# A two-layer hybrid block whose instruction order is planned with the frame's timeline simulation

## The chip, the cores and the metric

One core of one Trainium2 chip runs the whole kernel. The metric is device time in microseconds of one execution; the figure for a kernel is the median of its runs.

## The reference

Two layers over 512 tokens of width 1024, 256 of context and 256 latent, in fp32. Each layer is FFN, token mix, FFN. The mix sends one normalised input through a projection `w_in`, whose parts feed four branches and four sigmoid gates:

```python
h = modulate(rms_norm(x, g_pre), mod[:, :, 3 * j], mod[:, :, 3 * j + 1])
return x + FFN_RES_WEIGHT * mod[:, :, 3 * j + 2] * rms_norm(swiglu(h, w1, w3, w2), g_post)
...
h_lat = modulate(rms_norm(x_lat, norm_pre[layer, 1]), mod_lat[:, :, 3], mod_lat[:, :, 4])
ya_l, ya_c = s5_branch(zl[0], zc[0], *s5_p, with_ctx_out)
yb_l, yb_c = mla_branch(zl[1:4], zc[1:4], *mla_p, rope_b, with_ctx_out)
yc_l, yc_c = hgrn_branch(zl[4:9], zc[4:9], *hgrn_p, with_ctx_out)
yd_l, yd_c = gqa_branch(zl[9:12], zc[9:12], *gqa_p, rope_d, with_ctx_out)
...
merged = gates[:, :, 0] * (branches[0] @ w_branch[0])
for i in range(1, N_BRANCH):
    merged = merged + gates[:, :, i] * (branches[i] @ w_branch[i])
return merged @ w_out
```

After each sub-layer the result is normalised, scaled and added to `x`. Layer 1 gives only the latent tokens out.

## The kernel before

Activations lie transposed, 128 channels to a partition block and tokens along the free axis; a 1024-channel tensor is eight tiles of 128x512. Every large matrix product is made of three fp32r matmuls (`mm3`, L346 to L348): each operand is split into a high part, cast on ScalarE (ACT; `whi` L318 for weights, `hh` L566 for the input), and a low part, the difference, on VectorE (DVE; `wlo` L319, `hl` L567). Weights stream from HBM in pieces of 128x1024 through three raw buffers and four pairs of split buffers; a cast waits until the matmuls that read its buffer's last piece are through.

The program is a sequence of FFN, mix, FFN, twice. Between two of them stands a `turn`: the last pieces of the old output are multiplied for the first half of the tokens and then for the second; for each half the sums of squares (`sqa` L587, L593) go through ones-matmuls (`st` L304) into a small tile; two reciprocal square roots of eleven operations of 128x2 each (L292 to L297, three rounds of Newton) follow one another, with `sx` (L616 to L619) between them; their results are spread over the partitions by matmuls (`rb` L311) and copied by ACT (`rbs` L313). Then `x` is updated (`ay` L632, `x` L633) and the next input is made (`ht` L564, `hh` L566, `hl` L567), eight blocks of each:

```python
t = self.u("ht")
nc.vector.scalar_tensor_tensor(
    t[:, a:b], self.x[kb][:, a:b], sc[:, kb, v : v + 1], rs, op0=ALU.mult, op1=ALU.mult)
nc.scalar.activation(hh[:, a:b], t[:, a:b], AF.Identity, bias=sh[:, kb, v : v + 1])
nc.vector.scalar_tensor_tensor(
    hl[:, a:b], t[:, a:b], sh[:, kb, v : v + 1], hh[:, a:b].bitcast(F32), op0=ALU.add, op1=ALU.subtract)
```

The first four pieces of the next stage's weights are loaded and split ahead of their use (`self.ahead`, L319 inside the turn). There are four full turns, and a last one with the latent half alone. In the mix, each branch is a lane of short matmuls with ACT and DVE steps between them; the gate projections (`pj`, 24 matmuls of 256 columns a piece in layer 1) are written between the lanes' steps as fillers. HGRN runs in two directions (`hgrn0`, `hgrn1`): in a direction, `hs` and `hb` belong to the output norm of the one before, `ckt`, `cst`, `clv`, `cdg` to its chunks, `oc` is its output. The S5 branch ends with `s5o`, the transposes `yt`, a gate product `gz` and the branch product `br` (L346 to L348).

The code is written in one order, with a priority for each instruction. The frame (`tile.TileContext`) then plans, for each engine, the order in which its instructions stand in the engine's queue: it takes the instructions that are ready by its own idea of durations, the more urgent first. Each engine executes its queue in that order and waits on semaphores for the others. The profile's line L1869 is the place where the frame is opened.

## Time and profile before

| | |
|---|---|
| median of 3 runs | 2361.51 us (2357.76 to 2361.8) |
| the profiled execution | 2360.09 us, span 2358.2 us |
| mean granted TensorE clock | 0.983 of full |
| PE (TensorE) busy | 2266.5 us, 96% |
| DVE busy | 1635.1 us, 69% |
| ACT busy | 903.0 us, 38% |
| HBM traffic | 326.79 MB by DMA, mean 139 GB/s |

The span is the time from the first instruction to the last; the profiled execution's own time has 1.9 us more around it. A share is an average over stages, and PE's records overlap where matmuls are pipelined.

### The profile page before, as it was taken

The numbers are of one execution on the slowest core, as the hardware profiler recorded it, in microseconds if no ns is written. First come the engines' busy times: TensorE is split into PE (matmuls) and PEld (weight loads), VectorE is DVE, ScalarE is ACT, GpSimd is POOL, SyncE is SP. The second block draws the span as 40 slices with busy tenths as digits, with TensorE's granted clock in tenths as the row PEclk, the third lists the DMA queues.
The fourth block names the chain that finished last, engine by engine and source line by source line (L and its number), as shares of the span: only waits on it lengthen the run. The fifth ranks groups of instructions, "written<-read, shape, count | busy, mean of one in ns | idle before, by whom it ended". The sixth has DMA issues, their size and how long they took to land.

```text
span 2358.2 us, 38797 instructions
## 1 busy us (share of the span) xinstructions
PE 2266.5 (96%) x15188; PEld 1903.8 (81%) x15188; DVE 1635.1 (69%) x4024; ACT 903.0 (38%) x1548; POOL 53.3 (2%) x116
## 2 busy tenths in 40 slices
PE   7999999999999999989999999999998999998998
PEld 4778779977557778888887898888897877888997
DVE  5887675756665574899776468777767886777554
ACT  3322323454443323542332333232234564345443
POOL 0000020000000000000002000000000000000000
PEclk9999999999999999999999999999998999998999
DMA  7545554221541243235555325656533332454664
GB/s 245 174 156 162 187 179 130 83 86 55 173 138 41 86 148 94 72 126 161 187 189 155 100 81 164 192 171 194 173 117 92 102 112 64 150 171 128 185 186 134
DMA packets 105270, 326.79 MB, mean 139 GB/s; under 512 B 16192, under 2 KB 17984, under 8 KB 105088
## 3 DMA queue, kind: packets, MB, share of 16 engines
q1 hardware_dynamic: 96448, 306.00, 42.2%
q0 software_dynamic: 4032, 9.93, 1.2%
q10 hardware_dynamic: 4608, 8.39, 1.0%
q8 instruction: 119, 1.95, 0.3%
q14 instruction: 63, 0.52, 0.1%
HBM read 311.20 MB, written 15.17 MB: 138 GB/s over the span
## 4 chain that ended last, share of the span: by engine, by line
PE 82%; DVE 10%; DMA 3%; ACT 3%; issue 2%; SPq 0%; DVEq 0%; ACTq 0%
PE h L346 10%; PE h L348 10%; PE h L347 10%; PE y L346 6%; PE y L348 6%; PE y L347 6%; PE pj L346 5%; PE pj L348 5%; PE pj L347 5%; DVE wlo L319 2%; PE s L896 2%; DMA araw<-in_w_adaT_dram 2%; ACT whi L318 1%; PE od L923 1%; PE tk L348 1%
## 5 line engine op out<-in xcount | busy, mean ns | idle before, releaser
L318 ACT CAST whi<-raw 128x1024 fp32r<-128x1024 f32 x402 | 421.4, 1050 | 805.8 <-DMA raw<-in_ffn_dram 288.1
L319 DVE TENSOR_TENSOR wlo<-raw,whi 128x1024 fp32r<-128x1024 f32 x402 | 490.9, 1223 | 285.4 <-ACT whi L318 283.4
L346 PE MATMUL h<-hh,whi 128*128 128x512 f32 (+1 forms) x1472 | 526.4, 359 | 11.1 <-DVE gf L687 3.9
L348 PE MATMUL h<-hh,wlo 128*128 128x512 f32 (+1 forms) x1472 | 525.3, 358 | 8.6 <-DVE wlo L319 8.6
L347 PE MATMUL h<-hl,whi 128*128 128x512 f32 (+1 forms) x1472 | 524.4, 357 | 0.0
L346 PEld LDWEIGHTS h<-hh,whi 128*128 128x128 f32 x1472 | 281.3, 192 | 55.5 <-issue 4.4
L348 PEld LDWEIGHTS h<-hh,wlo 128*128 128x128 f32 x1472 | 281.3, 192 | 50.9 <-DVE wlo L319 8.8
L347 PEld LDWEIGHTS h<-hl,whi 128*128 128x128 f32 x1472 | 281.7, 192 | 38.2
L346 PE MATMUL pj<-hh,whi 128*128 128x256 f32 (+1 forms) x800 | 276.5, 348 | 3.3 <-ACT hh L566 2.7
L348 PE MATMUL pj<-hh,wlo 128*128 128x256 f32 (+1 forms) x800 | 274.3, 345 | 4.4 <-DVE wlo L319 4.4
L347 PE MATMUL pj<-hl,whi 128*128 128x256 f32 (+1 forms) x800 | 275.3, 345 | 0.0
L346 PE MATMUL y<-gh,whi 128*128 128x256 f32 (+1 forms) x726 | 240.7, 332 | 2.8 <-ACT t L686 2.5
L348 PE MATMUL y<-gh,wlo 128*128 128x256 f32 (+1 forms) x726 | 241.2, 332 | 0.0
L347 PE MATMUL y<-gl,whi 128*128 128x256 f32 (+1 forms) x726 | 240.7, 332 | 0.0
L348 PEld LDWEIGHTS pj<-hh,wlo 128*128 128x128 f32 x800 | 153.7, 193 | 24.9 <-DVE wlo L319 6.0
L346 PEld LDWEIGHTS pj<-hh,whi 128*128 128x128 f32 x800 | 153.9, 193 | 23.5 <-issue 5.2
L347 PEld LDWEIGHTS pj<-hl,whi 128*128 128x128 f32 x800 | 154.2, 193 | 18.4 <-issue 3.9
L346 PEld LDWEIGHTS y<-gh,whi 128*128 128x128 f32 x726 | 137.9, 190 | 16.2 <-ACT t L686 2.7
L348 PEld LDWEIGHTS y<-gh,wlo 128*128 128x128 f32 x726 | 137.9, 190 | 13.0
L347 PEld LDWEIGHTS y<-gl,whi 128*128 128x128 f32 x726 | 137.9, 190 | 12.9
L425 DVE SCALAR_TENSOR_TENSOR aj<-araw,cr 128x512 f32<-128x512 f32 x112 | 77.2, 689 | 55.4 <-DMA araw<-in_w_adaT_dram 55.0
L688 ACT CAST gh<-gf 128x512 fp32r<-128x512 f32 (+1 forms) x88 | 49.8, 566 | 148.4 <-DVE gf L687 148.1
(413 smaller groups left out, 3263.0 us busy)
## 6 DMA issues: line engine op xcount, KB each, us to landing
raw<-in_ffn_dram SPq DMA_DIRECT2D x267, 512.0 KB, 4.0
araw<-in_w_adaT_dram SPq DMA_DIRECT2D x104, 512.0 KB, 4.1
raw<-in_win_dram SPq DMA_DIRECT2D x102, 512.0 KB, 3.7
araw<-in_w_ada_dram SPq DMA_DIRECT2D x24, 512.0 KB, 3.8
raw<-in_wout_dram SPq DMA_DIRECT2D x17, 512.0 KB, 3.6
raw<-in_wbr_dram SPq DMA_DIRECT2D x16, 512.0 KB, 3.7
araw<-in_w_ada_dram SPq DMA_DIRECT2D x22, 256.0 KB, 5.5
s5G<-s5g POOLq DMA_DIRECT2D x16, 256.0 KB, 3.1
```

Of the source, the lines that this page charges most:

```text
L318: self.nc.scalar.copy(hi, src)
L319: self.nc.vector.tensor_tensor(lo, src, hi.bitcast(F32), op=ALU.subtract)
L346: mm(ps, wh, xh, start=start, stop=False, skip_group_check=True)
L347: mm(ps, wh, xl, start=False, stop=False, skip_group_check=True)
L348: mm(ps, wl, xh, start=False, stop=stop, skip_group_check=True)
L425: nc.vector.scalar_tensor_tensor(w if v else junk, w, 1.0, S[v], op0=ALU.mult, op1=ALU.mult, accum_out=t[:, 2 * op + i, v : v + 1])
L688: nc.scalar.copy(gh[:, a:b], gf[:, a:b])
L896: nc.tensor.matmul(s[:, :w], q[:, j * P : (j + 1) * P], k[:, :w], start=True, stop=True)
L923: nc.tensor.matmul(out[n][64 * h : 64 * h + 64, j * P : (j + 1) * P], vh(kb), ph[:, kb * P : (kb + 1) * P], start=kb == 0, stop=kb == nk - ...
```

## The change

```diff
-    with tile.TileContext(nc) as tc:
+    with tile.TileContext(nc, schedule_with_timeline_sim=True) as tc:
         build(tc, aps, out)
```

The instructions, tiles, pools and priorities stay as they are. The frame's plan now takes the times of its timeline simulation, so the queues come out in another order: on PE 13066 matmuls in both, on DVE 3592 instructions, on SyncE 672 DMAs. Three places follow.

The first place is DVE's queue in the turn behind the first FFN (the first turn). In the order before, the second reciprocal square root stands between the updates of `x`; the numbers behind the names are buffers, and `wlo_3753` is a weight of the old stage:

```order
L616 TENSOR_TENSOR sx_3620<-st_3594,ry_3602 128x2
L617 SCALAR_TENSOR_TENSOR sx_3620<-st_3594,sx_3620 128x2
L319 TENSOR_TENSOR wlo_3753<-raw_3750,whi_3752 128x1024
L618 TENSOR_TENSOR sx_3620<-sx_3620,ry_3602 128x2
L632 TENSOR_TENSOR ay_2842<-ay_2842,rbs_3615 128x256
L619 SCALAR_TENSOR_TENSOR sx_3620<-sx_3620,sx_199 128x2
L632 TENSOR_TENSOR ay_2854<-ay_2854,rbs_3615 128x256
L292 TENSOR_SCALAR rs_3625<-sx_3620 128x2
L633 TENSOR_TENSOR x_107<-x_107,ay_2842 128x256
L293 TENSOR_SCALAR ry_3626<-rs_3625 128x2
L633 TENSOR_TENSOR x_108<-x_108,ay_2854 128x256
L295 TENSOR_TENSOR rt_3627<-ry_3626 128x2
```

Still before, farther down in the same turn, the splits for the next stage (`wlo_3893`, `wlo_3899`, `wlo_3905`) stand behind the first half's last `hl`:

```order
L567 SCALAR_TENSOR_TENSOR hl_3588<-ht_3828,mod_3_642,hh_3587 128x256
L610 TENSOR_SCALAR sv_3846<-st_3838 128x2
L319 TENSOR_TENSOR wlo_3893<-raw_3890,whi_3892 128x1024
L567 SCALAR_TENSOR_TENSOR hl_3590<-ht_3834,mod_3_642,hh_3589 128x256
L292 TENSOR_SCALAR rs_3848<-sv_3846 128x2
L319 TENSOR_TENSOR wlo_3899<-raw_3896,whi_3898 128x1024
L293 TENSOR_SCALAR ry_3849<-rs_3848 128x2
L319 TENSOR_TENSOR wlo_3905<-raw_3902,whi_3904 128x1024
```

In the new order, at the place of the first of these pieces:

```order
L616 TENSOR_TENSOR sx_3620<-st_3594,ry_3602 128x2
L319 TENSOR_TENSOR wlo_3893<-raw_3890,whi_3892 128x1024
L617 SCALAR_TENSOR_TENSOR sx_3620<-st_3594,sx_3620 128x2
L618 TENSOR_TENSOR sx_3620<-sx_3620,ry_3602 128x2
L619 SCALAR_TENSOR_TENSOR sx_3620<-sx_3620,sx_199 128x2
L292 TENSOR_SCALAR rs_3625<-sx_3620 128x2
L293 TENSOR_SCALAR ry_3626<-rs_3625 128x2
L295 TENSOR_TENSOR rt_3627<-ry_3626 128x2
L296 SCALAR_TENSOR_TENSOR rt_3627<-rt_3627,sx_3620 128x2
L319 TENSOR_TENSOR wlo_3899<-raw_3896,whi_3898 128x1024
L297 SCALAR_TENSOR_TENSOR ry_3626<-rt_3627,ry_3626 128x2
L632 TENSOR_TENSOR ay_2842<-ay_2842,rbs_3615 128x256
```

Two of those splits now stand inside the second root, whose small operations follow one another, and the eight L632 stand in one run behind them. The other two splits come between the L633 that follow; then come eight `ht` in a row and behind them the eight `hl`. The other three full turns read the same way, that behind the first mix a little differently.

The second place is PE's queue in layer 1's mix, at the start of the second HGRN direction. Before:

```order
L346 MATMUL pj_18043<-hh_16013,whi_18039 128x256
L347 MATMUL pj_18043<-hl_16014,whi_18039 128x256
L348 MATMUL pj_18043<-hh_16013,wlo_18040 128x256
L346 MATMUL pj_18043<-hh_16015,whi_18039 128x256
L1150 MATMUL ckt_17701<-cst,ckd_17681 128x128
L347 MATMUL pj_18043<-hl_16016,whi_18039 128x256
L348 MATMUL pj_18043<-hh_16015,wlo_18040 128x256
L1150 MATMUL ckt_17701<-cst,ckd_17681 128x128
L346 MATMUL pj_18043<-hh_16017,whi_18039 128x256
L347 MATMUL pj_18043<-hl_16018,whi_18039 128x256
L1150 MATMUL ckt_17701<-cst,ckd_17681 128x128
L348 MATMUL pj_18043<-hh_16017,wlo_18040 128x256
```

And in the new order, from the norm of the direction before:

```order
L346 MATMUL pj_18467<-hh_16021,whi_18463 128x512
L347 MATMUL pj_18467<-hl_16022,whi_18463 128x512
L348 MATMUL pj_18467<-hh_16021,wlo_18464 128x512
L865 MATMUL hb_17620<-cst,he_17621 128x128 x2
L1150 MATMUL ckt_17701<-cst,ckd_17681 128x128 x3
L1155 MATMUL cst_17707<-vc_16671,ckt_17702 64x64 x4
L1155 MATMUL cst_17707<-vc_16673,ckt_17702 64x64 x2
L1201 MATMUL clv_17754<-cx_17748 64x64
L1201 MATMUL clv_17755<-cx_17748 64x64
L1201 MATMUL clv_17754<-cx_17748 64x64
L1201 MATMUL clv_17755<-cx_17748 64x64
L1201 MATMUL clv_17775<-cx_17769 32x32 x4
```

The `pj` that stood between the `ckt`, `cst`, `clv` and `cdg` now stand ahead of `hb`; from there to the last `oc` there is none.

The third place is PE's queue at the end of layer 1's S5 branch. Before, the last `gz` is followed by 47 `pj` and then `br`:

```order
L347 MATMUL gz_19659<-yl_19646,gwh_19628 128x256
L348 MATMUL gz_19659<-yh_19645,gwl_19629 128x256
L347 MATMUL pj_20314<-hl_16008,whi_20310 128x256
L348 MATMUL pj_20314<-hh_16007,wlo_20311 128x256
L346 MATMUL pj_20314<-hh_16009,whi_20310 128x256
L347 MATMUL pj_20314<-hl_16010,whi_20310 128x256
```

In the new order `br` follows at once:

```order
L348 MATMUL gz_19649<-yh_19645,gwl_19629 128x256
L347 MATMUL gz_19659<-yl_19646,gwh_19628 128x256
L348 MATMUL gz_19659<-yh_19645,gwl_19629 128x256
L346 MATMUL br_20387<-yh_20373,whi_20383 128x256
L346 MATMUL br_20396<-yh_20373,whi_20383 128x256
L346 MATMUL br_20405<-yh_20373,whi_20383 128x256
L347 MATMUL br_20387<-yl_20374,whi_20383 128x256
```

The same holds for the two joints ahead of it, from `s5o` to `yt` and from `yt` to `gz`: the five last groups of `pj` stand ahead of the last `s5o`.

## Rows read from the trace of the kernel before

**Rows 1.** The page: busy time by engine, and the chain that ended last.
```profile
PE 2266.5 (96%) x15188; PEld 1903.8 (81%) x15188; DVE 1635.1 (69%) x4024; ACT 903.0 (38%) x1548; POOL 53.3 (2%) x116
...
PE 82%; DVE 10%; DMA 3%; ACT 3%; issue 2%; SPq 0%; DVEq 0%; ACTq 0%
```

**Rows 2.** Turn windows: us; busy us (count) of PE, PEld, DVE, ACT, POOL; PEclk.
```profile
416.00:452.00 36.00, 31.32 (x245) 30.59 (x245) 33.46 (x121) 12.96 (x25) 1.32 (x3) 0.95 0.25 78
990.00:1029.00 39.00, 31.20 (x239) 30.68 (x239) 37.26 (x132) 16.23 (x34) 0.00 (x0) 0.87 0.22 68
1381.00:1417.00 36.00, 31.41 (x241) 30.67 (x240) 32.86 (x119) 12.75 (x25) 0.00 (x0) 0.91 0.26 74
1756.00:1793.00 37.00, 27.00 (x198) 26.01 (x197) 33.30 (x120) 12.77 (x25) 1.32 (x3) 0.85 0.25 76
2135.00:2165.00 30.00, 22.43 (x126) 20.55 (x125) 25.51 (x80) 11.42 (x24) 0.00 (x0) 0.66 0.28 88
```

**Rows 3.** Waits of PE: waited for, total us, times, longest us.
```profile
PE h L348 <- DVE wlo L319: 8.6, 2, 6.5
```

**Rows 4.** Timeline of DVE, first turn: start us, us, engine and line.
```profile
416.69 0.16 DVE L292 TENSOR_SCALAR rs<-sv 128x2 int32<-128x2 int32 x1
...
418.93 0.16 DVE L616 TENSOR_TENSOR sx<-st,ry 128x2 f32<-128x2 f32 x1
...
419.89 1.23 DVE L319 TENSOR_TENSOR wlo<-raw,whi 128x1024 fp32r<-128x1024 f32 x1 [0.61 <-ACT whi L318]
...
425.91 0.16 DVE L297 SCALAR_TENSOR_TENSOR ry<-rt,ry 128x2 f32<-128x2 f32 x1
...
425.98 0.76 DVE L632 TENSOR_TENSOR ay<-ay,rbs 128x256 f32<-128x256 f32 x2
...
426.65 0.76 DVE L633 TENSOR_TENSOR x<-x,ay 128x256 f32<-128x256 f32 x2
...
427.34 1.28 DVE L564 SCALAR_TENSOR_TENSOR ht<-x,mod,rbs 128x256 f32<-128x256 f32 x3
...
436.09 1.22 DVE L319 TENSOR_TENSOR wlo<-raw,whi 128x1024 fp32r<-128x1024 f32 x1
```

**Rows 5.** Timeline of PE, first turn.
```profile
431.40 0.28 PE L348 MATMUL y<-gh,wlo 128*128 128x256 f32 x1
...
437.37 0.58 PE L348 MATMUL pj<-hh,wlo 128*128 128x256 f32 x1 [2.13 <-DVE wlo L319]
...
451.84 0.74 PE L346 MATMUL pj<-hh,whi 128*128 128x256 f32 x4 [1.17 <-ACT hh L566]
```

**Rows 6.** Windows: a turn's first half, a stall, HGRN, S5 tail.
```profile
437.40:448.90 11.50, 11.50 (x85) 11.50 (x86) 10.35 (x41) 1.42 (x2) 1.32 (x3) 0.86 0.63 194
1010.60:1020.80 10.20, 5.10 (x24) 5.10 (x25) 9.66 (x30) 2.97 (x5) 0.00 (x0) 0.50 0.33 92
1890.60:1936.00 45.40, 43.87 (x588) 36.47 (x588) 39.52 (x122) 30.73 (x80) 0.00 (x0) 1.00 0.38 115
2088.80:2111.20 22.40, 22.31 (x188) 21.78 (x185) 14.73 (x22) 13.89 (x25) 0.00 (x0) 1.00 0.59 176
```

**Rows 7.** Groups by form in the HGRN stretch of layer 1: busy, mean.
```profile
L348 PE MATMUL pj<-hh,wlo 128*128 128x256 f32 x65 | 19.0, 293 | 0.3 <-DVE wlo L319 0.3
...
L346 PE MATMUL pj<-hh,whi 128*128 128x512 f32 x11 | 4.5, 414 | 0.6 <-ACT gt L1676 0.6
...
L319 DVE TENSOR_TENSOR wlo<-raw,whi 128x1024 fp32r<-128x1024 f32 x10 | 12.2, 1220 | 1.1 <-ACT whi L318 1.0
```

**Rows 8.** Timelines of ACT and PE, S5 tail of layer 1.
```profile
2089.08 0.59 ACT L1617 ACTIVATE sq<-s5o 64x512 f32<-64x512 f32 x1 [0.47 <-PE s5o L1611]
...
2109.62 0.72 ACT L321 ACTIVATE yh<-gsg 128x256 fp32r<-128x256 f32 x2
...
2111.19 0.28 PE L346 MATMUL br<-yh,whi 128*128 128x256 f32 x1
```

**Rows 9.** Timeline of PE, layer 0, first br of S5.
```profile
944.59 0.96 PE L346 MATMUL br<-yh,whi 128*128 128x512 f32 x3 [1.92 <-ACT yh L321]
```

## Prediction

> **What bounds the kernel now.** I read the page first. TensorE (PE) is busy 2266.5 of 2358.2 us, VectorE (DVE) 1635.1, and 82% of the chain that ended last is PE [rows 1]. So the kernel is a PE stream with 91.7 us of holes, and an order that adds or takes away holes moves the end one for one; work that only changes place inside a full stretch is worth nothing. The view by windows then says where the holes are: the four full turns and the short last one hold 4.7 + 7.8 + 4.6 + 10.0 + 7.6 = 34.7 us of them, and there DVE is the fuller engine: 33.5 of 36 us, 37.3 of 39, 32.9 of 36, 33.3 of 37 [rows 2]. The longest single wait for a weight split lies in a turn, 6.5 us of PE's h matmuls [rows 3]. The other 57 us are thin: the first weights, the two mixes, the last output. In two stretches of layer 1's mix that the new order touches, PE has almost no hole: 43.87 of 45.4 us in the HGRN stretch, 22.31 of 22.4 in the S5 tail [rows 6].
>
> **The turn, in DVE's queue.** The change adds no work: the same instructions stand on PE and DVE. In a turn it moves four 128x1024 splits (wlo, L319) from behind the first half's hl to a place among the small rsqrt operations and the x updates; it puts all eight ht ahead of the first hl; and it takes the small operations out from between the large ones. I walk the first turn through.
>
> Prices [rows 4]: the eleven operations of a rsqrt, each waiting for the last, take 418.93 - 416.69 = 2.24 us, 0.20 each; one small operation ahead of a large one costs 0.07 (425.91 to 425.98); four large ones (L632, L633) take 427.34 - 425.98 = 1.36, 0.34 each; of three ht in 1.28 us each adds 0.40, and hl has the same shape; a split busy for 1.2 us adds about 1.14 to the queue. From ry's last operation to the first ht, through rb on PE and the copy on ACT, is 427.34 - 425.91 = 1.4 us.
>
> The first split of the stretch starts at 419.89 in both orders, since it waits for ACT's cast [rows 4]. Between it and the last operation of the second rsqrt the new order has five splits (5.7 us), the eleven (2.2), twelve more bare small ones (2.4), and 24 large ones, 16 of the update and 8 of the other half's sums (8.2): 18.5 us, so ry is there at 438.4. Then 1.4 to the first ht, 3.2 for eight ht, 0.3 to the first hl: **443.3**. Before, PE's stream on the first half began at 437.37, released by the split of 436.09 [rows 4, 5]: +6. The last y matmul starts at 431.40 [rows 5] and would stand about there in the new order too; behind it the new order has nothing for PE but stat matmuls, so this hole grows from some 6 us to 12.
>
> The second half: eight hl (3.2), ten bare small operations of its first rsqrt (2.0), about ten more around the second (2.0), 16 large ones (5.4), 1.4 to ht and 3.2 for eight ht: 443.3 + 17.2 = 460.5 against 451.84 before [rows 5]. So the turn ends **8 us later**. The work of the first half cannot cover this: it was 11.5 us long [rows 6], and 443.3 + 11.5 is 454.8, so PE waits a second time. Bounds: below, DVE's list holds only about 2 us more work ahead of the second half's hl (the two late halves of the eight ht), which would be all if the small operations found cover; above, +12, if the casts, which wait for PE to release weight buffers, hold the splits up, since everything in DVE's queue stands behind a split whose cast is late. I take +8 for the turns at 416, 1381 and 1756, whose lists read alike; +6 at 990, where the old order already lost 6.5 us at the split [rows 3]; +3 at 2135, which has only one half. **Sum 33, from 12 to 50.**
>
> On the small operations there is a rule to weigh. The row gives 0.20 for a bare one and 0.07 for a covered one, so each that loses its cover costs 0.13. The Trainium skill (Perfetto Trace Analysis, Optimizing Scalar/DVE Operations) says that DVE's fixed access cost is about 60 ns on SBUF and that the profiled latency is about twice this, because the second half overlaps the next instruction; by this a bare one would cost an estimated 0.06 more than a covered one, and the some 20 of a turn 1.2 us in place of 2.6. The rows decide here.
>
> **HGRN in layer 1.** In the old order, from 1890.6 to 1936, PE works on gate projections (pj) between the lane's short matmuls: three groups of 64 or 65 matmuls of 256 columns and three of 10 or 11 of 512, of which one each is shown [rows 7]. At 22.31 us for 188, 0.119 us a 256-column matmul [rows 6], and double that for 512, that is (193 + 2 x 31) x 0.119 = 30 of the 45.4 us. In the new order the pj are used up ahead of hb, and behind it PE has only the lane's own matmuls to the last oc. DVE's work of the lane is 39.5 us less ten splits of 1.14 (12.2 us busy) [rows 6, 7], about 28; PE's own is 43.9 - 30 = 14, beside some 6 us of pj between hs and hb. So PE waits at least 28 - 14 - 6 = 8 us, and more through hops between engines; less the 1.5 idle of before, I take **+12 (5 to 18)**.
>
> **S5 tail in layer 1.** Before, pj matmuls stand between the last s5o and yt, yt and gz, and gz and br, so the chain of small ACT and DVE steps from the first ACT step at 2089.08 to br at 2111.19 costs PE nothing [rows 6, 8]. In the new order all of these pj are ahead of the last s5o. The bare chain is 16 steps on ACT and DVE of 0.4 to 0.7 us (the first is 0.59, the last two 0.72 together [rows 8]), some of them side by side; as steps in a row about 8.5 us, plus yt and gz, of which PE works 2.5. **+8 (6 to 10).**
>
> **Layer 0's mix** gives its pj out early in the same way; there PE waited 1.92 us ahead of br in the old order [rows 9], and a bare gz-to-br chain and thinner cover at the end of the attention lane make this 3 to 10: **+5 (0 to 10)**.
>
> **The clock.** After the stall at 990 the granted clock was 0.50 for 10.2 us, that is 1.2 GHz, while PE was 5.1 us busy [rows 6]; half of that busy time, 2.6 us, is the loss. The holes of three turns grow past that stall, so I add **3 (0 to 8)** in all.
> The Trainium skill (TensorE: Matmul & The Clock Gate, Part 1) puts it as a default that is throttled and that activity releases; by it every longer hole is followed by a stretch at half rate, and the trace agrees: 0.85 to 0.95 in the turns, 1.00 in the stretches without a hole [rows 2, 6].
>
> **What may come back.** Fillers that run earlier close holes earlier. The 57 us outside the turns are the limit; the first weights and the last output can't be closed by order. I credit **10 (0 to 25)**. Front matter (the first 60 us), the S5 tables and the long FFN stretches I cost at nothing: in FFN stretches PE keeps its order, and around the tables FFN matmuls cover them; if that cover failed, it would be a few us.
>
> **Sum.** 33 + 12 + 8 + 5 + 3 - 10 = 51. On the profiled execution's own 2360.1 us that is 2411; the median of the three runs is 2361.5, 1.4 above it, which I leave out. **Predicted 2411 us, +2.2%.**
>
> **Rivals.**
> - *The turns alone.* The mixes gain at one end what they lose at the other, since pj that move forward fill holes there: 33 + 3 = 36, **2396 us**. For it: DVE has room in the mixes. Against it: the stretch of rows 6 had no hole to fill.
> - *Everything bare.* Turns at 12, HGRN at 18, tail 10, layer 0 at 10, clock 8, nothing back: about +80, **2440 us**. For it: DVE is the fuller engine in a turn, and casts hold it.
> - *Faster.* Fillers close 25 us of the thin holes, and in a turn only the 2 us of DVE work that moved ahead of the second half count, because the small operations find cover: 4 x 2 + 8 - 25 = -9, **2351 us**. It needs the turn's loss below about 3 us and HGRN's stall swallowed by earlier pj. Against it: the walk, and only 57 us of which most are at the ends.
> - *No change.* The queues run ahead of each other enough that order in a list does not bind: **2360 us**. Against it: the wait of 6.5 us at a split shows that it binds.
>
> **Chances.** The forecast's case 0.36, turns alone 0.27, everything bare 0.20, no change 0.06, faster 0.11. About 0.2% is what measurement of this kernel can tell: faster 0.11, same 0.06, slower 0.83. The range for 8 in 10 reaches from just under the case of the turns alone, with those at their lower bound, to everything bare: 2372 to 2442.
>
> **What would show it.** In the new trace each full turn has a PE hole of 10 us or more behind the last y matmul, ended by DVE's ht or hl (not by wlo), and a second one ahead of the second half; the wait for the split in the turn at 990 is gone. Around the second HGRN direction of layer 1, and ahead of br in layer 1, PE sits idle 10 and 8 us. The FFN stretches stay full. I am wrong if the turn's stream starts within 3 us of where it did, or if the mixes show fewer holes than 57 us less the ends.

## The result, and the profile after

The changed kernel takes 2551.02 us (median of 4 runs, 2549.94 to 2554.05) against 2359.78 (4 runs) for the kernel before on the same chip: ratio 1.0803, 95% interval 1.0785 to 1.0821, 191 us more. The forecast was 2411, its range ended at 2442: the direction was right, the size was not. The span of the profiled execution is 2547.9 us.

The page of the changed kernel: busy time by engine, and the granted clock in 40 slices, in tenths.

```profile
PE 2323.2 (91%) x15188; PEld 1958.5 (77%) x15188; DVE 1640.6 (64%) x4024; ACT 894.8 (35%) x1546; POOL 53.2 (2%) x116
...
PEclk9999999998888989989999989999998988997999
```

The same 15188 PE instructions are busy 56.7 us longer than in [rows 1], and PE's holes are 2547.9 - 2323.2 = 224.7 us where they were 91.7. So 133 us of the loss are holes and 57 are longer busy time of the same instructions. PE's waits in the changed kernel, by what it waited for (total us, times, longest us):

```profile
PE st L304 <- DVE sqa L587: 34.7, 5, 10.5
...
PE h L346 <- DVE gf L687: 12.4, 3, 8.2
PE pt L908 <- DVE e L903: 10.2, 6, 2.6
...
PE cdg L1229 <- DVE cx L1188: 5.8, 3, 2.3
...
PE h L348 <- DVE wlo L319: 4.7, 4, 1.6
```

The first answers to the turns: the second half's sums (sqa) now end the hole behind the last y. The wait of 6.5 us for a split in [rows 3] is gone, as forecast. But gf is a wait in the FFN, and pt and cdg are steps of attention and HGRN lanes in the mixes. In the kernel before, the same waits were these; those for adaev and for yh were the two largest in layer 0's mix:

```profile
PE st L304 <- DVE sqa L587: 8.5, 10, 2.6
...
PE h L346 <- DVE gf L687: 3.9, 2, 2.2
...
PE adat L452 <- DVE adaev L449: 2.2, 2, 1.6
PE br L346 <- ACT yh L321: 1.9, 1, 1.9
...
PE cdg L1229 <- DVE cx L1188: 0.4, 1, 0.4
...
PE pt L908 <- DVE e L903: 0.2, 1, 0.2
```

To see where it went, both traces were cut at the same PE instructions. Lengths in us, with what the holes and the busy time of PE gained, and the prediction's own term:

| stage | before | after | holes | busy | forecast |
|---|---|---|---|---|---|
| first 400 us | 400.1 | 406.4 | +7.7 | -1.4 | 0 |
| five turns | 304.8 | 351.9 | +32.9 | +14.2 | +33 |
| layer 0's mix | 493.6 | 562.0 | +48.1 | +20.4 | +5 |
| two FFN stretches | 658.1 | 686.5 | +16.0 | +12.4 | 0 |
| layer 1's mix | 308.5 | 348.8 | +27.1 | +13.1 | +20 |
| last FFN | 184.8 | 182.8 | 0 | -2.0 | 0 |

The clock stood in the forecast as +3 and holes closed elsewhere as -10. The table's holes add up to 132 and its busy time to 57; the output behind the last FFN takes 1.2 us longer. The windows of the changed kernel behind it (us; busy us and count of PE, PEld, DVE, ACT, POOL; granted clock; DMA's busy share and GB/s): layer 0's mix, a lane of it, the two FFN stretches, then the second HGRN direction and the S5 tail of layer 1.

```profile
481.50:1043.50 562.00, 503.06 (x3896) 382.33 (x3894) 292.82 (x666) 191.06 (x372) 4.37 (x13) 0.91 0.29 90
...
680.00:700.00 20.00, 14.70 (x235) 9.99 (x237) 9.37 (x26) 6.05 (x13) 0.00 (x0) 0.76 0.06 15
...
1135.60:1479.70 344.10, 332.89 (x1694) 278.61 (x1693) 234.18 (x599) 107.96 (x149) 20.77 (x40) 0.99 0.49 154
1539.40:1881.80 342.40, 333.25 (x1576) 279.42 (x1575) 239.69 (x535) 101.80 (x136) 0.00 (x0) 0.98 0.54 170
...
2062.10:2097.30 35.20, 24.03 (x399) 17.63 (x398) 30.19 (x110) 21.13 (x67) 0.00 (x0) 0.71 0.16 48
2279.50:2293.20 13.70, 5.26 (x23) 4.29 (x21) 6.48 (x14) 5.79 (x13) 0.00 (x0) 0.69 0.11 43
```

And layer 0's mix and the second FFN stretch of the kernel before:

```profile
463.80:957.40 493.60, 482.75 (x3908) 361.23 (x3907) 297.34 (x672) 194.22 (x375) 4.55 (x13) 0.99 0.33 102
...
1420.00:1745.10 325.10, 325.10 (x1565) 274.79 (x1564) 241.85 (x538) 103.14 (x139) 0.00 (x0) 1.00 0.58 180
```

**The walk through the first turn holds.** The y matmuls ahead of this turn stand 6.35 us later in the new trace (the same matmul at 403.64 and 397.29). DVE in the changed kernel, the end of the list that the prediction walked (start us, us):

```profile
443.82 0.16 DVE L297 SCALAR_TENSOR_TENSOR ry<-rt,ry 128x2 f32<-128x2 f32 x1
446.61 3.26 DVE L564 SCALAR_TENSOR_TENSOR ht<-x,mod,rbs 128x256 f32<-128x256 f32 x8 [2.62 <-ACT rbs L313]
...
449.85 0.47 DVE L567 SCALAR_TENSOR_TENSOR hl<-ht,mod,hh 128x256 fp32r<-128x256 f32 x1
```

Less 6.35, ry is done at 437.6 (walked: 438.4) and the first hl starts at 443.5 (443.3). Two misses of about a microsecond cancel in this: ry came 0.8 us early, and three operations of its root were not bare but stood among the updates and sums farther down the list; and from ry's last operation to the first ht it took 2.8 us, not 1.4, since rb stands behind the sums on PE's queue. PE in the same place:

```profile
436.61 0.28 PE L348 MATMUL y<-gh,wlo 128*128 128x256 f32 x1
...
443.24 1.86 PE L304 MATMUL st<-cst,sqa 128*128 128x1 f32 x8 [6.35 <-DVE sqa L587]
444.96 1.20 PE L311 MATMUL rb<-cst,ry 128*128 128x128 f32 x4
...
450.38 0.58 PE L347 MATMUL pj<-hl,whi 128*128 128x256 f32 x1 [1.47 <-DVE hl L567]
...
466.10 0.74 PE L346 MATMUL pj<-hh,whi 128*128 128x256 f32 x4 [1.52 <-ACT hh L566]
```

The last y is followed by 6.35 us of nothing, then by sums and rb, and the stream starts at 450.38, that is 444.0 where [rows 5] had 437.37; the second half comes at 466.10, that is 459.8 (walked: 460.5).

### The profile page after: what moved, and what is told of

Its sections match the earlier page's. It is cut to its first block, busy times and chain, and to the rows that moved or that the text cites. A ratio compares the mean times of both kernels' runs of the same rounds, so it can differ in the third digit from the quotient of the medians.

```text
span 2547.9 us, 38848 instructions
## 1 busy us (share of the span) xinstructions
PE 2323.2 (91%) x15188; PEld 1958.5 (77%) x15188; DVE 1640.6 (64%) x4024; ACT 894.8 (35%) x1546; POOL 53.2 (2%) x116
## 5 line engine op out<-in xcount | busy, mean ns | idle before, releaser
L346 PE MATMUL h<-hh,whi 128*128 128x512 f32 (+1 forms) x1472 | 530.6, 363 | 24.0 <-DVE gf L687 12.4
L347 PE MATMUL h<-hl,whi 128*128 128x512 f32 (+1 forms) x1472 | 530.5, 361 | 8.1 <-DVE hl L567 8.1
L425 DVE SCALAR_TENSOR_TENSOR aj<-araw,cs 128x512 f32<-128x512 f32 x96 | 65.7, 684 | 73.2 <-DMA araw<-in_w_adaT_dram 72.2
```

The lines of the kernel that those rows point to most:

```text
L346: mm(ps, wh, xh, start=start, stop=False, skip_group_check=True)
L347: mm(ps, wh, xl, start=False, stop=False, skip_group_check=True)
L425: nc.vector.scalar_tensor_tensor(w if v else junk, w, 1.0, S[v], op0=ALU.mult, op1=ALU.mult, accum_out=t[:, 2 * op + i, v : v + 1])
```

## The experiments

Most kernels below hold queues in a given order: after the program is written, each instruction of a queue gets an ordering link to the one ahead of it that adds no semaphore. The diff against the kernel before is this one, with another table each time:

```diff
+def pin(tc, nc):
...
+        queue = [queue[k] for k in itertools.accumulate(steps)]
+        for first, then in zip(queue, queue[1:]):
+            tc.add_manual_dep(then, first.name, behind, reason="pin")
...
         build(tc, aps, out)
+        pin(tc, nc)
```

**Where the loss lies.** The theory: each stage loses by its own order. The rival: a stage pays for what another one moved. Four kernels hold all five queues: the old order, with one kind of stage in the new order.

> The old order in every queue, except that the instructions which the old kernel executed between 463.7 and 957.3 us (layer 0's mix) stand among themselves in the new order. Theory A (each stage's own order costs what the stage grew by in the new kernel's trace): the stage grew from 493.6 to 562.0 us, so +68, near 2428 us, with PE idle about 45 us more and the rest of the growth as busy time at a lower granted clock. Rival B (the mix grew because weights and fillers reached it late from the changed FFN and turn ahead of it): at most +25. Rival C (the prediction's own term for this mix): +5.

Measured: 2433.88 us, ratio 1.0314 (1.0278 to 1.0350), +75.

> The old order, except that what the old kernel executed in the four turns and the short last one (400 to 463.7, 957.3 to 1035, 1368 to 1420, 1745 to 1807.3 and 2115.9 to 2165 us) stands in the new order. Theory A (local): the growth of these stages in the new kernel's trace is 11 + 15 + 8 + 8 + 6 = 47, near 2407 us. The prediction's sum for them with its clock term: +36. Rival B (half of the growth comes with the new order around the turn): +24 or less.

Measured: 2404.83, 1.0199 (1.0168 to 1.0230), +46.

> The old order, except that what the old kernel executed between 1807.3 and 2115.9 us (layer 1's mix) stands in the new order. Theory A: +40, near 2400 us, made of a gain of some 17 in the first 130 us and a loss of some 57 behind it. The prediction's terms for HGRN and the S5 tail: +20. Rival B: under +15.

Measured: 2401.05, 1.0185 (1.0149 to 1.0222), +42.

> The old order, except that the first 400 us and the FFN stretches (1035 to 1368, 1420 to 1745, behind 2165 us) stand in the new order. Theory A: +33, near 2393 us, with waits of PE for gf (L687) and for splits, since DVE's queue has the tables and modulation work of later stages ahead of them. The prediction: 0, because PE's own order hardly changes there.

Measured: 2390.15, 1.0133 (1.0104 to 1.0161), +31. The four add up to 194 of the 191 us, and a stage left in the old order kept its length: with layer 0's mix in the new order the turns took 304.3, layer 1's mix 309.0, the FFN stretches 656.5. For the turns and both mixes the theory holds by stage too: alone they grow by 45, 71 and 39 us, in the changed kernel by 47, 68 and 40. For the FFN it holds in part: alone, the two stretches grow by 16 us, not 28, and the first 400 us by 12, not 6 (where they keep their old order, in the three other runs, they took 395.4 to 400.0). So the sum of 194 fits better than its FFN part. The FFN's share has one main line in the run with that stage alone, longer than in the changed kernel; 12.4 of the 14.8 us lie in the first 400:

```profile
PE h L346 <- DVE gf L687: 14.8, 4, 7.8
```

**What is late in a turn.** The splits that stand early on DVE's queue, or the order of the sums and updates?

> The old order everywhere, except that the five turns have the new order of every engine's queue, and of that the weights' splits, casts and loads (L318, L319, L327) stay at their old places. With the splits at their new places the turns alone cost +46 (2404.8), and the wait of st for DVE's sqa was 35.1 us in 5 waits. Theory A (the splits that stand ahead of the second half's sums on DVE's queue are what is late): the wait of st falls under 10 us and the time is 2365 to 2380. Rival B (the sums are late because the updates and the sums themselves are reordered, the splits only fill the time): the wait of st stays at 25 to 35 us and the time is 2395 to 2410.

Measured: 2431.96, 1.0311 (1.0286 to 1.0337), +74. Neither: it got 27 us worse than the whole new turn. PE's waits in it:

```profile
PE st L304 <- DVE sqa L587: 23.9, 5, 7.5
PE h L346 <- ACT whi L318: 21.1, 3, 9.9
...
PE pj L346 <- ACT whi L318: 9.7, 1, 9.7
```

The sums are still 24 us late without the splits (35.1 with the whole new turn), and now the splits and casts are late too, because the new order of PE's queue asks for them early. The converse, the splits alone, only VectorE's queue held, here in the first turn:

```diff
 L616 TENSOR_TENSOR sx_3620<-st_3594,ry_3602 128x2
+L319 TENSOR_TENSOR wlo_3893<-raw_3890,whi_3892 128x1024
 L617 SCALAR_TENSOR_TENSOR sx_3620<-st_3594,sx_3620 128x2
-L319 TENSOR_TENSOR wlo_3753<-raw_3750,whi_3752 128x1024
 L618 TENSOR_TENSOR sx_3620<-sx_3620,ry_3602 128x2
```

> VectorE's queue is fixed: the old order everywhere, only with the turns' weight splits (L319) at the places that the new order gives them, earlier among the updates; the other queues are planned around it by the default durations. Theory A (splits ahead of the sums are what makes the second half's sums late): TensorE's waits for wlo (13.0 us before) go, but its waits for sqa grow from about 1 us a turn by 2 to 4 us each, and the time is 2362 to 2380. Rival (the splits only fill time in which the sums' inputs are not there yet): the waits for wlo go, nothing else moves, and the time is 2345 to 2356, below the kernel before.

Measured: 2390.52, 1.0125 (1.0105 to 1.0146), +31. The waits for wlo went (0.3 us is left), but it is not the sums that became late:

```profile
PE rb L311 <- DVE ry L297: 26.0, 13, 6.0
...
PE st L304 <- DVE sqa L587: 3.9, 2, 3.0
```

A split of 1.2 us among the small steps delays the reciprocal square root, and PE waits at rb. So the splits, moved early in the old order, cost 31 us through the norm chain. That is no share of the turns' 46, since the new turn without them was not cheaper. Does the chain at its old places then mend the new turn?

> The five turns in the new order (2404.8 alone), but in the four full ones the first half's norm chain stands at its old places: VectorE's short steps of 0.16 us (L610, L292 to L297, L616 to L619), TensorE's rb (L311) and ScalarE's copy rbs (L313). In the first turn that copy came at 435.2 us with the whole turn in the new order, after the second half's sums, and at 426.9 before, under the last y. Theory C (the first half's h is late because its chain's short steps stand between the long block updates and its rb behind the second half's sums): rbs is done before the last y ends, and the updates of h start at the end of the sums instead of 2.8 us later: 2388 to 2398. Rival (only the sums are late, the chain has time): 2401 to 2410.

Measured: 2434.01, 1.0314 (1.0294 to 1.0334), +75, again worse than the whole new turn. PE waits in it 32.4 us for ry at rb, in 10 waits, and 23.2 for sqa: rb now stands ahead of the sums on PE, while DVE still has the new list's splits ahead of ry. The edit replaced one wait by another, so it doesn't tell whether the late chain alone costs time, and that stays open. What it shows, with the run without splits, is that a turn's new order can't be half undone.

**The clock.** Matmuls whose result nobody reads go into PE's holes in the old order; they write columns of a PSUM tile that nothing uses.

```diff
             self.stat(s2, n, post["xa"], (a, b))
+            if v:
+                for _ in range(next(self.counts, 0)):
+                    self.warm.append(nc.tensor.matmul(s2[:, 256:], self.ident, self.cst[:, :256],
+                                                      start=True, stop=True, skip_group_check=True).ins)
```

> The old order of every queue, with matmuls of 256 columns whose result nobody reads put into TensorE's holes behind the last sums of the four full turns: 5, 14, 4 and 4 of them, which adds work and no result. Theory A (a hole of 2 to 6.5 us is followed by a stretch at half the granted clock: 437.1, 1010.6, 1399.7 and 1775.2 us, 3.4 to 10.2 us long, some 27 us in all): the stretches go, busy time of the other matmuls falls by 7 to 13 us, and the time is 2347 to 2355. Rival B (the clock falls for the fill as well, or the fill itself is in the way of the next piece): 2360 to 2372.

Measured: 2358.42 (12 runs) against 2357.56, ratio 0.9994 (0.9981 to 1.0007): no change. The window of the second turn (columns as above) shows what it did to the clock:

```profile
985.00:1024.00 39.00, 35.78 (x270) 33.92 (x269) 35.82 (x128) 16.46 (x34) 0.00 (x0) 1.00 0.22 68
```

PE's timeline behind the fill shows what it did to the time:

```profile
1013.45 0.39 PE L348 MATMUL h<-hh,wlo 128*128 128x256 f32 x1 [0.37 <-DVE wlo L319]
1013.68 0.28 PE L346 MATMUL h<-hh,whi 128*128 128x256 f32 x1
```

The same place in the kernel before:

```profile
1015.70 0.58 PE L348 MATMUL h<-hh,wlo 128*128 128x256 f32 x1 [6.52 <-DVE wlo L319]
1016.08 0.41 PE L346 MATMUL h<-hh,whi 128*128 128x256 f32 x1
1016.29 0.41 PE L347 MATMUL h<-hl,whi 128*128 128x256 f32 x1
```

The granted clock is 1.00 where [rows 2] had 0.87, and the matmuls behind the hole stand 0.12 us apart, not 0.21. But h still starts when DVE's split is there, 7.57 us behind the last sums in both traces (1005.88 to 1013.45 here, 1008.13 to 1015.70 before). The faster stretch ends in a longer wait for DVE: PE's waits for ry at rb are 8.9 us instead of 6.5, and rb starts 11.9 us behind the last sums where it started 12.2. In this turn a clock kept up is worth nothing, since DVE sets the pace. It is the one turn of the four that shows this: in the others, with 4 or 5 matmuls each, a stretch at half the clock was still there behind the hole, 6.8, 3.4 and 3.4 us long where it had been 3.4, 6.8 and 6.8.

**Which queue carries it.** First a blunt test: PE's queue in each mix, with the turn behind it, held in the order in which the code is written, once under each plan.

```diff
+        queue = [i for i in list(self.nc.cur_bb.bb.instructions)[first:] if str(i.engine).endswith(".PE")]
...
+        for a, b in zip(queue, queue[1:]):
+            self.tc.add_manual_dep(b, a.name, behind, reason="written order")
```

> The changed kernel, with TensorE's queue held in the order in which the code is written from the first to the last instruction of each layer's mix, the turn behind it included; the other queues are planned by the timeline simulation within that. To be read against its twin with the default durations. Theory A (the mixes lose by the order of TensorE's queue, whole pieces of filler ahead of ready steps): the two twins differ only by what the FFN stretches and the turns that end them cost, 55 to 70 us. Rival B (it is the order on VectorE and ScalarE that makes the steps late): the twins differ by 150 us or more. No level is forecast for either, since neither planner has made this queue.

Measured: 2714.66, 1.1510 (1.1485 to 1.1535).

> The kernel before, with TensorE's queue held in the order in which the code is written from the first to the last instruction of each layer's mix, the turn behind it included; the twin of the kernel above. Theory A: 55 to 70 us below its twin. Rival B: 150 us or more below it. If the planner's order of TensorE's queue is worth nothing at all, this one is within 1% of the kernel before.

Measured: 2638.66, 1.1189 (1.1160 to 1.1218). They differ by 76 us, near theory A's 55 to 70 and far from 150. The second also shows what the planner's order of PE's queue in the mixes is worth under the default durations: 281 us. But both are so slow that PE's order could hide what the other queues do, so it was tried in layer 0's mix alone, one queue held at a time.

> TensorE's queue has the new order in layer 0's mix and the old one elsewhere, fixed; the queues of the other engines are planned around it by the default durations (VectorE's then differs from that of the kernel with the whole mix in the new order in 537 lines). With all queues of that mix in the new order the time was 2433.9, +75. Theory A (the mix loses by TensorE's order, whole pieces of filler ahead of ready steps): 2415 to 2440. Rival B (it loses by the order on VectorE and ScalarE): 2365 to 2395.

Measured: 2446.46, 1.0371 (1.0347 to 1.0395), +87.

> The same with VectorE's queue fixed instead: the new order in layer 0's mix, the old one elsewhere; TensorE's queue and the others are planned around it by the default durations (TensorE's then differs from that of the kernel with the whole mix in the new order in 1352 lines). Theory A: 2365 to 2395. Rival B: 2415 to 2440. If both this and its twin lie at 2415 or more, either queue's order is enough for the loss, since the lanes cross from one engine to the other.

Measured: 2429.09, 1.0292 (1.0271 to 1.0314), +70. The third case came true: either queue's new order is enough, with the other queues planned around it. Theory A in its first form falls. Then the whole program, one queue held and the rest planned by the other plan.

> The changed kernel (planned with the timeline simulation), but TensorE's queue is fixed in the order that it has in the kernel before, from the first instruction to the last; VectorE's and ScalarE's are planned around it (VectorE's differs from the changed kernel's in 2524 lines, from that of the kernel before in 3898). Theory A (TensorE's order carries the loss): 2365 to 2420, and layer 0's mix is within 15 us of before. Rival B (the order on VectorE and ScalarE makes the steps late whatever TensorE's is): 2470 to 2550, with long waits of TensorE for VectorE at lane steps.

Measured: 2482.28, 1.0512 (1.0486 to 1.0539), +121.

> The counterpart: the default durations, but TensorE's queue is fixed in the order that it has in the changed kernel. Theory A: 2510 to 2570. Rival B: 2380 to 2450.

Measured: 2541.61, 1.0766 (1.0747 to 1.0785), +180.

> The changed kernel, but VectorE's queue is fixed in the order that it has in the kernel before; TensorE's is planned around it by the timeline simulation (4748 lines from the changed kernel's, 4972 from that of the kernel before). Theory A: the simulation still has TensorE's order to choose, and most of the loss stays: 2460 to 2550. Rival B: 2365 to 2420. If this and the run with TensorE's old order both fall under 2420, the order of either queue is enough to hold the program.

Measured: 2566.19, 1.0875 (1.0836 to 1.0914), +205. VectorE's old order saves nothing in the total. PE's new order alone brings nearly the whole loss, as theory A had it; but PE's old order takes only some 70 of the 191 us away, which is rival B's range. By stage it is clearer. Layer 0's mix, the FFN stretch behind the second turn and layer 1's mix, with PE's queue old and the others newly planned:

```profile
486.00:1004.90 518.90, 494.99 (x3908) 368.90 (x3907) 296.99 (x672) 197.29 (x379) 4.55 (x13) 0.96 0.30 97
1090.80:1432.90 342.10, 331.60 (x1692) 277.22 (x1691) 235.15 (x599) 108.24 (x149) 20.76 (x40) 1.00 0.48 155
...
1899.00:2234.50 335.50, 308.26 (x2866) 265.61 (x2865) 227.31 (x587) 156.84 (x335) 4.36 (x13) 0.96 0.35 112
```

With PE's queue new and the others planned by the default durations:

```profile
476.20:1051.80 575.60, 506.81 (x3896) 385.28 (x3895) 294.21 (x666) 191.60 (x373) 4.43 (x13) 0.90 0.27 88
1142.90:1476.90 334.00, 329.61 (x1693) 276.29 (x1693) 235.09 (x599) 107.92 (x149) 20.76 (x40) 1.00 0.49 159
...
1924.30:2293.40 369.10, 318.41 (x2871) 277.52 (x2871) 232.70 (x588) 156.74 (x332) 4.29 (x13) 0.88 0.31 102
```

Before, they took 493.6, 333.0 and 308.5. Layer 0's mix loses 25 us by the other queues and 82 by PE's, layer 1's mix 27 and 61, where the changed kernel lost 68 and 40; the FFN stretch loses 9 by the other queues and 1 by PE's. So PE's order is the costlier one in both mixes, but in layer 1's the other queues alone already bring two thirds of the change's loss; the FFN's loss is not PE's; the turns lose by either (+41 and +33). The run with VectorE's old order agrees on the FFN and hides it in its total: its turns lose 31 us where they lost 47, and its FFN stretches 5 where they lost 28, the second of them without a hole,

```profile
1547.90:1874.40 326.50, 326.50 (x1576) 276.29 (x1575) 242.96 (x541) 104.33 (x141) 0.00 (x0) 1.00 0.56 179
```

but its mixes, with PE's queue planned anew around the old one of VectorE, lose 92 and 64.

**What it is in PE's order.** The filler of a mix is ada (the modulation's matmuls, adaps and adat), gate (pj) and branch (br) work. PE's queue in layer 0's mix has it in 115 runs of 9.2 matmuls before, in 84 of 12.6 after. This piece of the difference, at 525 us in the new trace, shows gate matmuls gathered ahead of a lane's step (cdg):

```diff
+L346 MATMUL pj_4575<-hh_3583,whi_4571 128x512
+L347 MATMUL pj_4575<-hl_3584,whi_4571 128x512
+L348 MATMUL pj_4575<-hh_3583,wlo_4572 128x512
...
 L1229 MATMUL cdg_4600<-cx_4594 32x32
```

Later in the same mix a lane runs with nothing between its steps. PE in the changed kernel:

```profile
690.20 0.81 PE L1229 MATMUL cdg<-cx 64*32 64x32 f32 x64 [2.30 <-DVE cx L1188]
...
697.68 1.87 PE L842 MATMUL hs<-cst,bs 128*128 128x1 f32 x8 [3.00 <-ACT bs L1002]
...
710.98 2.79 PE L443 MATMUL adaps<-araw,cS 128*32 128x256 f32 x24
```

Two waits of 2 to 3 us, and then 12 ada matmuls (24 records) in one piece. From this cdg to the adat ahead of that piece, the changed kernel takes 20.2 us for 91 lane matmuls with no filler between them; the kernel before took 20.1 us for the same 91 with 38 filler matmuls between them. Before, and then in the changed kernel, columns as above:

```profile
639.00:659.00 20.00, 17.98 (x222) 12.49 (x220) 12.78 (x43) 7.40 (x16) 0.00 (x0) 1.00 0.45 143
...
690.20:710.40 20.20, 15.64 (x175) 11.73 (x175) 13.21 (x44) 7.13 (x19) 0.00 (x0) 0.51 0.00 1
```

The lane got no faster by standing alone, and its own matmuls ran at half the clock; the filler's time has to be paid elsewhere. Whether the bare lane would be faster at full clock was not tried. The test makes such runs in the old order and moves nothing but filler on PE:

```diff
 L347 MATMUL pj_4377<-hl_3580,whi_4373 128x512
-L348 MATMUL pj_4377<-hh_3579,wlo_4374 128x512
 L346 MATMUL pj_4338<-hh_3587,whi_4334 128x512
...
 L348 MATMUL pj_4405<-hh_3579,wlo_4402 128x512
+L348 MATMUL pj_4377<-hh_3579,wlo_4374 128x512
```

> The old order, but in layer 0's mix the filler matmuls (ada, gate and branch pieces) are held back on TensorE's queue until 8 (up to 585 us) or 16 (from 680 us) of them stand together; the lanes' steps keep their order, and the other queues are planned around it by the default durations. It makes 81 runs of filler, 13.1 matmuls long in the mean, where the kernel before has 115 of 9.2 and the changed one 84 of 12.6. Theory A (the lumps themselves: between two of them the lane runs bare): 2400 to 2440, with TensorE's idle time in that mix up by 25 to 50 us. Rival C (it is which steps the lumps stand ahead of, and weights that are not there yet; lumps behind the ready steps cost little): 2355 to 2385.

Measured: 2394.30, 1.0154 (1.0127 to 1.0180), +33, between the two cases. Layer 0's mix in it, by windows:

```profile
466.00:991.90 525.90, 485.60 (x3908) 366.49 (x3907) 297.64 (x672) 193.69 (x375) 4.55 (x13) 0.97 0.30 96
```

PE's longest waits there:

```profile
PE pt L908 <- DVE e L903: 8.3, 5, 2.1
PE cdg L1229 <- DVE cx L1188: 5.2, 2, 2.9
```

The holes of the mix grew from 10.9 to 40.3 us, inside what theory A expected, and the same waits came that the change brought (pt for e, cdg for cx), of which the kernel before had none this long. So lumps of this size, with the lanes' steps in their old order and the other queues planned around them, cost the mix 32 us where the change costs it 68. The other half was not separated: which lumps stand ahead of which step, what weights are late there, or the order of the lanes' steps among themselves. The last is a rival that the queues make plain: of the mix's 1428 lane matmuls the changed kernel has 352 at another place among themselves and this run none, while the run with VectorE's new order alone, which loses 71 us in this mix, has 333 at another place and its filler in 103 runs of 10.3, nearly as before. So lumps are not the only way to this loss.

No version that beats both kernels was found; the one with filled holes ties with the kernel before.

## Why the prediction was wrong

**Right, with their sizes.** The walk through the turn, to within 1 us of ry and hl. The turns: 33 forecast, +32.9 measured in holes, and 47 with the busy time. By turn the holes grew by 7.1, 8.1, 7.1, 5.8 and 4.9 us where 8, 6, 8, 8 and 3 stood, so the sum fits better than its parts, which is luck. The HGRN stretch of layer 1: +12 forecast, and the window from 2062.1 has 35.20 - 24.03 = 11.2 us of holes, where the stretch had 1.5 before [rows 6]. The S5 tail: +8 forecast, 13.70 - 5.26 = 8.4 measured. The wait for the split at 990 is gone. In one point the mechanism was another one: the hole behind the last y is ended by the second half's sums first, and only then by ht or hl; and of the five waits for sums only the longest, 10.5 us, reaches the 10 us that each full turn was to show.

**The step that failed: layer 0's mix at +5 (0 to 10).** It measured +48 us of holes, and 68 with the longer busy time (71 with this mix alone in the new order). The prediction read one wait there, 1.92 us ahead of br [rows 9], and priced a bare chain at that place. It used the walk's method (what is left between the steps when the filler moves) on two stretches of layer 1 and not on layer 0's lanes, where the filler moves in the same way in many more places. The waits are short, at most 5 us each, so none of them stands out; together they are the largest term.

**The clock at +3 (0 to 8).** The busy time grew by 57 us. The price was taken from one stall in a turn [rows 6] and applied to three turns; the clock fell in the mixes and in the FFN as well. By the clock records inside the span, PE was granted half the clock in 11 stretches of 77.8 us in sum before, and in 30 of 304.3 us after. This is not a cost to be added freely to the holes: in the turn at 990 the faster matmuls bought nothing. How much of the mixes' 33 us of busy growth would come back at full clock was not tried.
The Trainium skill (TensorE: Matmul & The Clock Gate, HAM oscillation — how this bites in real kernels) takes the loss as half of the throttled time; by it the 226.5 us more would be an estimated 113 us, and the measured growth of 57 decides.
In part the difference is idle time: PE was busy in 53.6 us of those stretches before and in 214.2 after, 160.6 more, and half of that is 80. Nor is everything that runs there twice as slow: in the lane above an s matmul (two records) took 1.12 us at full clock and 2.07 at half, but 64 cdg records 0.76 and 0.89.

**The FFN stretches and the first 60 us at nothing.** "In FFN stretches PE keeps its order" was nearly true and did not suffice: with PE's new order and the others as before planned, the two stretches lose 3 us, while VectorE's and ScalarE's newly planned queues cost them 18 with PE's old one. The tables, which FFN matmuls were to cover, and the modulation work move on DVE's queue, and gf comes late behind them: in the first 400 us DVE is mostly at s5s, s5x and aj until gf starts at 131.23, and PE waits 8.2 us for it. Measured: +28 in the two stretches, +6 in the first 400 us.

**The credit of 10.** No stage gave it back. Layer 1's mix is 17.0 us ahead after its first lane, only because PE has done less of its filler by then (110.8 us busy where it was 126.1); the rest of that mix gives it back and 40 more.

**Of the rivals**, everything bare (2440) was nearest in kind. It was too low, since it kept layer 0 at 10 and the clock at 8; its sum is also short by its own terms, for the turns' upper bound of 50 with 18, 10, 10 and 8 makes 96, not 80, and the range ended where this rival stood. In the terms of the 51 that make 2411: layer 0 is 43 short, the clock 54, the FFN and the start 24, the credit 10, layer 1's mix 7; with them it is 2549.

## What to carry to other kernels

When a planner's durations change, every stage that hides lane latency under filler must be walked, not only the ones that show a wait now: count the filler between two lane steps in the old and the new order, and price the step bare. The order of the queues is one thing: three kernels that undid only a part of the new order (the splits, the norm chain, VectorE's queue) were slower in total than with all of it, so a plan is judged by stage and each stage undone as a whole. A stage where no wait stands out can still hold the largest term, as the sum of many.

## What was not expected of the hardware

Filling one of PE's holes with 14 matmuls kept the granted clock at 1.00 through the turn at 990, with the following matmuls 0.12 us apart instead of 0.21, and the kernel's time did not move (0.9994); 4 or 5 matmuls in the three other turns did not keep it there. Over the whole program 226.5 us more at half the clock went with 57 us more of busy time: PE was busy in 160.6 of them, and short matmuls such as cdg lost little (0.76 to 0.89 us for 64 records).
